# Hybrid attention trunk on one core: where two activation tables come from, when unit 0's heads take ScalarE, and how one matmul triple in a step reads its moving operand

## The chip, the core and the metric

The kernel runs on one core of a Trainium2 chip. The core has TensorE (matmuls), VectorE, ScalarE (activations and copies), GpSimd and SyncE; the last two mostly issue DMAs. In profile rows they are PE (its weight loads PEld), DVE, ACT, POOL and SP. The metric is the time of one execution on the device in microseconds; three executions of the kernel before took 1690.44, 1692.59 and 1696.43 us.

## What is computed

Only layer 0 of the reference exists (DEPTH is 1): an RMSNorm, an attention branch with a residual, and a last RMSNorm. There are 256 rows of 4096 floats, 32 heads of 128.

```python
h = x + attn_branch(rms_norm(x, norm_attn), w_in_attn, w_out_attn)
out = rms_norm(h, final_norm)
# attn_branch: q, k, v, g = split(xn @ w_in, 4)          w_in is 4096 x 16384
z = einsum(q_block, k) * scale                           # one head, strictly causal
log_fail = where(causal, log_sigmoid(-z), 0)
suffix = cumsum(log_fail, axis=3, reverse=True) - log_fail
a = exp(log_sigmoid(z) + suffix)                         # 0 where not causal
o = a @ v
branch = (o * silu(g)) @ w_out                           # w_out is 4096 x 4096
```

All is float32, and the two projections are nearly all of the work.

## The kernel before

**Projections.** Twenty units follow each other on TensorE: units 0 to 15 make columns of q, k, gate and v, two heads each, and units 16 to 19 multiply by w_out. A unit has 16 steps along the contraction. A step works on 2 x 2 blocks; in units 0 and 16 ("plain") it takes 8 products, in the others ("mixed") 7 products in 11 or 9 of the 16 steps, made from sums and differences of blocks (SEVEN_PARTS), and 8 in the rest. One product is a **triple** of matmuls: weights and activations are each split into a rounded high part and a low rest (wh, wl; sh, sl or oh, ol), and the triple is wh with sh, wl with sh, wh with sl, all into one PSUM bank (acc). The weights are the moving operand, 512 columns wide. ScalarE casts the raw weights to wh, VectorE subtracts to get wl and also forms the sums.

**How a triple reads.** mm3 (lines 816 to 822) gives each matmul a read and write order by a letter: with "e" the 512 columns go in groups of eight neighbours, four passes over the row ("128x4x16x8" in the order of instructions), with "c" in groups of four ("128x4x32x4"). product (from line 1245) picks the three letters: the first seven triples behind a heads' group use BEHIND_OTHERS (line 36), else the first triple of a step uses IN_STEP (line 37, by the step's number, even or odd), and all others "eee".

**Heads.** While unit u + 1 runs, the two heads of unit u are worked off between its triples. One head is four groups on TensorE (turn: the transposes; scores; scan: the sums of f, high and low part fh and fl; values) and between them work on ScalarE: a copy, softplus and its scaled copy (f), a cast (fh), Relu and Exp (a), small copies. Each unit also takes one Silu of the gate. Silu, softplus and Exp are in three table sets, so a load of a table (ACT_TABLE_LOAD) stands ahead of Silu, and ahead of softplus and Exp of each head: five a unit, 80 in 16 units. The last heads' group of a unit stands in step 6 of the next one.

**What sets the order.** A planner (class Plan) runs the whole program through costs written in it and emits the instructions in the order that results. Each piece of work for ScalarE or VectorE waits in a heap under a key, a time, and the lowest key goes first. act and dve use soon(), 4 us ahead of TensorE's place, if none is given (lines 327 to 339); casts of weights have the time of their first product, less 2 or 6 us. What the planner emits is fixed: the chip runs each engine's instructions in that order, and each waits for its operands.

**The output part and the end.** plain_h (from line 1075) is unit 16's end: four copies from PSUM to h, one for each bank. The last parts of unit 19 are reordered so that banks 5, 4, 2 and 3 are finished one after the other. With each, block_done adds the bank, ScalarE takes squares with a sum (sq), VectorE joins the sums, and finish (from line 1184) takes r = Exp(-0.5 * Ln(mean)), a Newton step on VectorE, and then the rows of the output are scaled and stored. It does so for rows 128 to 255 first and for rows 0 to 127 after the last bank. Ln and Exp come from different sets there, so each of the two root() calls has a table load ahead of Ln and one ahead of Exp. One load at the program's begin (line 274) asks for a set that has both; the first norm's factor uses it.

All instructions pass through one helper, so the profile gives line 133 for nearly all of them; they are told apart by operation and tile.

Of the kernel before, what the change touches and what calls it, by code (L numbers as in the profile page):

```python
# [13 lines left out]
AF = mybir.ActivationFunctionType  # L14
# [5 lines left out]
P = 128  # L20
S = 256
# [11 lines left out]
EPS = 1e-6  # L33

RUNS = {"e": (4, 8), "c": (4, 4), "g": (2, 8)}
BEHIND_OTHERS = ("ccc", "ecc", "eee", "eee", "eee", "eee", "cce")
IN_STEP = ("cce", "ecc")
BEHIND = {}
WARM, IDLE = 10, 640

# [7 lines left out]
TABLE = 1400  # L48
# [17 lines left out]
H_LATER = 3  # L66
GAIN_LATER = 30.0
ON_SCALAR = ((1, 3, 5), (1, 3))
AHEAD, SUMS_AHEAD = 4.0, 4.0
BLOCKS_LATER = 2  # L70
FORMS_BEHIND = 3
# [34 lines left out]
def scalar_ns(n):  # L106
    return 98 + n / 1.2
# [142 lines left out]
def kernel(  # L250
# [10 lines left out]
    nc = Plan(tc)  # L261
# [14 lines left out]
    def minus(out_, full, part):  # L276
        nc.vector.tensor_tensor(out=out_, in0=full, in1=part.bitcast(F32), op=ALU.subtract)
# [49 lines left out]
    def soon(c=4.0):  # L327
        return nc.here + 1e3 * c


    def dve(emit, n, key=None, more=0, **kw):
        n = n if isinstance(n, tuple) else (n,)
        cost = sum(vector_ns(m) for m in n) + 122 * (len(n) - 1) + more
        return nc.work("vector", cost, emit, soon() if key is None else key, **kw)

    def act(emit, n, key=None, **kw):
        n = n if isinstance(n, tuple) else (n,)
        cost = sum(scalar_ns(m) for m in n) + 100 * (len(n) - 1)
        return nc.work("scalar", cost, emit, soon() if key is None else key, **kw)
# [3 lines left out]

    since_others, words = 0, BEHIND_OTHERS

    def ten(emit, *n, what):
        def others():
            nonlocal since_others, words
            first_ = BEHIND.get(what, ())
            since_others, words = 0, first_ + BEHIND_OTHERS[len(first_) :]  # L350
            emit()

        return nc.work("tensor", 40 + sum(tensor_ns(m) for m in n), others, nc.here - 1e4, wait=400)
# [453 lines left out]
    st, ev = {}, {}  # L807

    def gate(u):
        yield nc.until(("gv", u))  # L810
        g = st["gv", u][:, :, 0:CW]
        n = NT * CW
        yield act(lambda: nc.scalar.activation(g, g, AF.Silu), n + TABLE)
        nc.tell(("gate", u))

    def mm3(out_, a, b, start, stop, orders):
# [8 lines left out]
    BW = 3 * P  # L825
    not_before = off.broadcast_to([P, 2, P])

    def head(u, i):
        yield nc.take("att", "gh", sooner=True)
        tr = att.tile([P, 2, S], F32, tag="att", name=f"tr{u}_{i}")  # L830

        def turn():
            for k in range(2):
                for t in range(NT):
                    c = k * CW + i * P
                    nc.tensor.transpose(tr[:, k, t * P : (t + 1) * P], st["qk", u][:, t, c : c + P], ident)

        yield ten(turn, P, P, P, P, what=("turn", i))
        if i == HG - 1:
            nc.give("one")  # L840
        qk = wp.tile([P, 2, S], F32, tag="gh", name=f"qkT{u}_{i}", bufs=ROWS)
        yield act(lambda: nc.scalar.copy(qk, tr), 2 * S)
        nc.give("att")
        yield nc.take("att", sooner=True)
        bank = att.tile([P, W], F32, tag="att", name=f"z{u}_{i}")
        z, gT = bank[:, 0:BW], bank[:, BW:W]

        def turned(to, t):
            nc.tensor.transpose(to, st["gv", u][:, t, i * P : (i + 1) * P], ident)

        def scores():
            kw = dict(stop=False, skip_group_check=True)
            nc.tensor.matmul(z[:, 0:P], qk[:, 1, P:S], qk[:, 0, P:S], start=True, **kw)
            nc.tensor.matmul(z[:, P:BW], qk[:, 1, 0:P], qk[:, 0, :], start=False, **kw)
            diagonal = z[:, 0 : 2 * P].rearrange("p (a b) -> p a b", a=2)
            nc.tensor.matmul(diagonal, ident_b, not_before, start=False, **kw)

        yield ten(scores, *FULL_P, *FULL_S, 2 * P, what=("scores", i))
        nc.give("gh")
        yield nc.take("gh", sooner=True)  # L860

        f = wp.tile([P, BW], F32, tag="gh", name=f"f{u}_{i}", bufs=ROWS)

        def soft():
            nc.scalar.activation(f, z, AF.Softplus, scale=scale)
            nc.scalar.activation(f, f, AF.Copy, scale=1.0 / scale)

        yield act(soft, (BW + TABLE, BW))
        yield nc.take("gh", "gh", sooner=True)
        fh, fl = (wp.tile([P, BW], F32R, tag="gh", name=f"f{k}{u}_{i}", bufs=ROWS) for k in "hl")  # L870
        yield act(lambda: nc.scalar.copy(fh, f), BW)
        yield dve(lambda: minus(fl, f, fh), BW)
        nc.give("gh")

        if i == 0:
            yield nc.until(("gate", u))

        def scan():
            kw = dict(start=False, skip_group_check=True)
            nc.tensor.matmul(z, neg_tri, fh, stop=False, **kw)  # L880
            nc.tensor.matmul(z, neg_tri, fl, stop=False, **kw)
            nc.tensor.matmul(z[:, 2 * P : BW], neg_one, fh[:, 0:P], stop=False, **kw)
            nc.tensor.matmul(z[:, 2 * P : BW], neg_one, fl[:, 0:P], stop=True, **kw)
            turned(gT, 0)

        yield ten(scan, BW, BW, P, P, P, what=("scan", i))
        nc.give("gh", "gh")
        gated = st["gv", u][:, :, i * P : (i + 1) * P]
        yield nc.take("gh", sooner=True)
        a = wp.tile([P, BW], F32, tag="gh", name=f"a{u}_{i}", bufs=ROWS)  # L890


        def weights_of():
            nc.scalar.activation(a, z, AF.Relu, scale=-scale)
            nc.scalar.activation(a, a, AF.Exp, scale=-1.0)

        yield act(weights_of, (BW, BW + TABLE))
        yield act(lambda: nc.scalar.copy(gated[:, 0, :], gT), P)
        nc.give("att")
        yield nc.take("att", sooner=True)  # L900
        bank2 = att.tile([P, BW], F32, tag="att", name=f"o{u}_{i}")
        o, gT2 = bank2[:, 0:S], bank2[:, S:BW]
        v = lambda t: st["gv", u][:, t, CW + i * P : CW + (i + 1) * P]

        def out_of_head():
            kw = dict(skip_group_check=True)
            nc.tensor.matmul(o, v(0), a[:, P:BW], start=True, stop=False, **kw)
            nc.tensor.matmul(o[:, P:S], v(1), a[:, 0:P], start=False, stop=True, **kw)
            turned(gT2, 1)

        yield ten(out_of_head, *FULL_P, *FULL_S, P, what=("values", i))
        nc.give("gh")
        yield act(lambda: nc.scalar.copy(gated[:, 1, :], gT2), P)
        o2 = o.rearrange("p (t b) -> p t b", t=NT)
        yield dve(lambda: nc.vector.tensor_tensor(out=gated, in0=o2, in1=gated, op=ALU.mult), S)
        nc.give("att")
# [3 lines left out]
    def heads(u):  # L920
        nc.start(gate(u))
        yield nc.until(("qk", u))
        for i in range(HG):
            yield from head(u, i)

        nc.tell(("heads", u))
        spill[u] = dp.tile([P, 4, P], F32, name=f"spill{u}")
        there = spill[u].rearrange("p (i t) b -> p t i b", t=NT)
        here = st["gv", u][:, :, 0:CW].rearrange("p t (i b) -> p t i b", i=HG)

        def out_():
            for t in range(NT):
                nc.gpsimd.dma_start(there[:, t], here[:, t])

        yield moved("gpsimd", out_, [2 * P] * NT, soon(), after=lambda: (nc.give("two"), nc.tell(("spilled", u))))
# [47 lines left out]
    def make_room():  # L983
        nonlocal ep
        rooms.close()
        ep = ctx.enter_context(tc.tile_pool(name="last", bufs=1))
# [87 lines left out]

    def plain_h(u, c):
        yield nc.until(*(("spilled", v) for v in range(NB)), ("full", u, PLAIN["C11"]))
        make_room()
        for k in range(2):
            new_h(c + k)
        for k in range(2):  # L1080
            for t in range(NT):
                b = PLAIN[f"C{t + 1}{k + 1}"]
                yield nc.until(("full", u, b))
                yield act(lambda: nc.scalar.copy(hs[c + k, t], ev[u][b]), W, place_of[u + 1, 0] - 2e3)
                nc.give(f"b{b}")
        nc.tell(("C", u))
# [121 lines left out]
    def rows_out(c, t, f, key):  # L1208
        h = hs[c, t]
        if c >= NJ - 2:  # L1210
# [6 lines left out]
            )  # L1217
        elif c in ON_SCALAR[t]:
            yield act(lambda: nc.scalar.activation(h, h, AF.Copy, scale=f), W, key)
# [25 lines left out]
    def product(n, k):  # L1245
# [7 lines left out]
        elif p["i"] == 0 and k == 0:  # L1253
            orders = IN_STEP[p["s"] % len(IN_STEP)]
        since_others += 1
# [89 lines left out]
```

## Time and profile before

| | |
|---|---|
| median of three executions | 1692.59 us (1690.44 to 1696.43) |
| the profiled execution, its own time | 1690.6 us |
| its span, first to last instruction | 1688.9 us |
| TensorE busy | 1666.1 us, 99% |
| VectorE busy | 1611.2 us, 95% |
| ScalarE busy | 1268.8 us, 75% |
| table loads on ScalarE | 84 and the first one, 1283 ns each |
| DMA | 417 MB, 247 GB/s in the mean |

All durations in the text come from the one profiled execution; between its span and its own time lie 1.7 us, and the median of the three lies 2.0 above its own time. A row such as "L133 ACT CAST wh<-raw 128x1024 x2" is line, engine, operation, what is written from what, shape and count; in timeline rows the start and the duration in us stand ahead, and in brackets the idle time of the engine before it and who ended it. The chain of waits is followed back from the last instruction: each piece is the work or the wait without which the next could not have begun. A matmul's duration in a row overlaps the next one's; its pace is the distance of starts.

### The profile page before, as it was taken

To read this page: it belongs to the slowest core of one execution; us is meant where nothing else is said; L and a number is where in the kernel's file an instruction comes from. 1 tells how busy PE (TensorE), PEld (TensorE's weight loads), DVE (VectorE), ACT (ScalarE), POOL (GpSimd) and SP (SyncE) were. 2 spreads that over 40 slices of the span, in tenths; PEclk is the share of its full clock that TensorE was granted. 3 is DMA by queue.
4 is the path that set the end of the run, shared out by engine and by line. 5 is a ranking of instruction groups with operands and counts; after the bars stand their busy time and mean duration, and the time that the engine had idled before them with its cause. 6 is when DMAs were issued, how large, how long until landed. Compare 5 with 4: busy or idle time off the path is not lost.

```text
span 1688.9 us, 24974 instructions
## 1 busy us (share of the span) xinstructions
PE 1666.1 (99%) x7731; PEld 1409.2 (83%) x7731; DVE 1611.2 (95%) x1851; ACT 1268.8 (75%) x1668; POOL 365.8 (22%) x448
## 2 busy tenths in 40 slices
PE   9999999999999999999999999999999999999995
PEld 7888888888888888888888888888888888888884
DVE  8889999999999999999999999999999978999996
ACT  8886968686868696868686868787878766656665
POOL 0022222222222222222222222222222112212110
PEclk9999999999999999999999999999999999999998
DMA  9968898988897979797979798889888977979894
GB/s 338 349 177 252 230 261 222 259 227 257 228 265 212 274 202 281 199 285 206 272 215 265 215 260 227 247 235 251 231 249 239 291 247 239 274 223 275 249 307 148
DMA packets 253174, 417.22 MB, mean 247 GB/s; under 512 B 28784, under 2 KB 77168, under 8 KB 253040
## 3 DMA queue, kind: packets, MB, share of 16 engines
q1 hardware_dynamic: 194544, 354.24, 62.9%
q0 software_dynamic: 58208, 61.11, 21.9%
q8 instruction: 60, 0.98, 0.2%
q14 instruction: 74, 0.61, 0.1%
q10 hardware_dynamic: 288, 0.28, 0.1%
HBM read 407.13 MB, written 8.39 MB: 246 GB/s over the span
## 4 chain that ended last, share of the span: by engine, by line
PE 93%; DVE 4%; issue 1%; ACT 1%; DMA 1%; SPq 0%; DVEq 0%; ACTq 0%
PE acc L133 88%; PE z L133 3%; DVE wl L133 2%; PE o L133 1%; PE tr L133 1%; DVE h L133 1%; DVE raw L133 1%; DMA raw<-in_w_out_dram 0%; ACT wh L133 0%; DMA xres<-in_x_dram 0%; ACT L133 0%; DMA raw<-in_w_in_dram 0%; DVE wh L133 0%; SPq L133 0%; ACT sq L133 0%
## 5 line engine op out<-in xcount | busy, mean ns | idle before, releaser
L133 ACT CAST wh<-raw 128x1024 fp32r<-128x1024 f32 (+1 forms) x1019 | 936.5, 966 | 326.0 <-PE acc L133 139.3
L133 DVE TENSOR_TENSOR wl<-raw,wh 128x1024 fp32r<-128x1024 f32 (+1 forms) x830 | 989.8, 1219 | 42.8 <-ACT wh L133 19.5
L133 PE MATMUL acc<-wh,sh 128*128 128x512 f32 x2048 | 766.0, 387 | 0.4 <-ACT wh L133 0.4
L133 PE MATMUL acc<-wh,sl 128*128 128x512 f32 x1883 | 721.3, 383 | 0.0
L133 PE MATMUL acc<-wl,sh 128*128 128x512 f32 x1718 | 657.7, 383 | 2.2 <-DVE wl L133 2.2
L133 POOL DMA_DIRECT2D raw<-in_w_in_dram x330 | 284.0, 945 | 1003.5 <-DMA raw<-in_w_in_dram 409.6
L133 PEld LDWEIGHTS acc<-wh,sh 128*128 128x128 f32 x2048 | 384.7, 188 | 70.9 <-ACT wh L133 0.8
L133 PEld LDWEIGHTS acc<-wh,sl 128*128 128x128 f32 x1883 | 352.8, 187 | 63.8 <-DVE sl L133 0.6
L133 PEld LDWEIGHTS acc<-wl,sh 128*128 128x128 f32 x1718 | 322.5, 188 | 58.9 <-DVE wl L133 3.6
L133 DVE TENSOR_TENSOR raw<-raw 128x512 f32<-128x512 f32 x378 | 359.9, 952 | 4.6 <-DMA raw<-in_w_out_dram 1.4
L133 PE MATMUL acc<-wh,oh 128*128 128x512 f32 x512 | 192.1, 383 | 0.0
L133 PE MATMUL acc<-wh,ol 128*128 128x512 f32 x488 | 186.5, 382 | 0.0
L133 PE MATMUL acc<-wl,oh 128*128 128x512 f32 x464 | 177.5, 383 | 1.5 <-DVE wl L133 1.4
L133 DVE TENSOR_TENSOR wh<-raw,wh 128x512 fp32r<-128x512 f32 x189 | 129.3, 684 | 1.4 <-ACT wh L133 1.4
L133 PEld LDWEIGHTS acc<-wh,oh 128*128 128x128 f32 x512 | 96.0, 187 | 17.1
L133 ACT ACT_TABLE_LOAD x84 | 107.8, 1283 | 1.5
L133 PEld LDWEIGHTS acc<-wh,ol 128*128 128x128 f32 x488 | 91.4, 187 | 16.0
L133 PEld LDWEIGHTS acc<-wl,oh 128*128 128x128 f32 x464 | 87.0, 187 | 18.1 <-DVE wl L133 2.8
L133 POOL DMA_DIRECT2D raw<-in_w_out_dram x48 | 41.8, 971 | 161.5 <-DMA raw<-in_w_out_dram 49.9
L133 POOL DMA_DIRECT2D p<-spill x28 | 17.0, 648 | 100.0 <-DVE ol L133 63.8
L133 DVE SCALAR_TENSOR_TENSOR gv_sb<-acc,scalars,gv_sb 128x512 f32<-128x512 f32 x45 | 33.5, 745 | 0.0
L133 ACT CAST oh<-p 128x512 fp32r<-128x512 f32 (+3 forms) x47 | 21.2, 471 | 13.8 <-DVE p L133 13.1
(87 smaller groups left out, 709.5 us busy)
## 6 DMA issues: line engine op xcount, KB each, us to landing
raw<-in_w_in_dram SPq DMA_DIRECT2D x1024, 256.0 KB, 4.5
raw<-in_w_out_dram SPq DMA_DIRECT2D x256, 256.0 KB, 4.4
raw<-in_w_in_dram POOLq DMA_DIRECT2D x330, 128.0 KB, 4.9
p<-spill POOLq DMA_DIRECT2D x28, 256.0 KB, 4.4
raw<-in_w_out_dram POOLq DMA_DIRECT2D x48, 128.0 KB, 5.6
xr<-in_x_dram SPq DMA_DIRECT2D x16, 256.0 KB, 5.1
spill<-gv_sb POOLq DMA_DIRECT2D x32, 128.0 KB, 4.8
xres<-in_x_dram SPq DMA_DIRECT2D x16, 256.0 KB, 5.8
```

The source lines that it names most:

```text
L133: return self.tc.keep_in_program_order(getattr(self.engine, name)(*args, **kw))
```

## The change

Three things. (1) BEHIND_OTHERS's last entry and IN_STEP's first go from "cce" to "ecc": the triple's four-column groups move from the first two matmuls to the last two. In steps with odd numbers IN_STEP was "ecc" already. (2) In unit 0 the ScalarE work of gate and head gets a key 12 us ahead of TensorE's place instead of 4 (HEADS_FIRST); a higher key means later, so casts of weights get in front of it. In the other units it stays at 4. (3) plain_h emits a load of the set that has both Ln and Exp, behind the last heads.

```diff
-BEHIND_OTHERS = ("ccc", "ecc", "eee", "eee", "eee", "eee", "cce")
-IN_STEP = ("cce", "ecc")
+BEHIND_OTHERS = ("ccc", "ecc", "eee", "eee", "eee", "eee", "ecc")
+IN_STEP = ("ecc", "ecc")
...
+HEADS_FIRST = 12.0
...
     def gate(u):
+        act_ = lambda *w: act(*w, soon(4.0 if u else HEADS_FIRST))
...
-        yield act(lambda: nc.scalar.activation(g, g, AF.Silu), n + TABLE)
+        yield act_(lambda: nc.scalar.activation(g, g, AF.Silu), n + TABLE)
...
     def head(u, i):
+        act_ = lambda *w: act(*w, soon(4.0 if u else HEADS_FIRST))
...
-        yield act(soft, (BW + TABLE, BW))
+        yield act_(soft, (BW + TABLE, BW))
...
-        yield act(weights_of, (BW, BW + TABLE))
-        yield act(lambda: nc.scalar.copy(gated[:, 0, :], gT), P)
+        yield act_(weights_of, (BW, BW + TABLE))
+        yield act_(lambda: nc.scalar.copy(gated[:, 0, :], gT), P)
...
     def plain_h(u, c):
         yield nc.until(*(("spilled", v) for v in range(NB)), ("full", u, PLAIN["C11"]))
+        yield act(lambda: nc.scalar.preload_act_table_set("natural_log_exp_and_others"), TABLE)
         make_room()
```

The copies qk, fh and gated[:, 1, :] in head go from act to act_ as well. Three places show what the planner and the placing of loads make of it.

ScalarE at the beginning of unit 1, where unit 0's first head begins; wh36 and wh37 are the casts for the second half of unit 1's step 1, f0_0 is softplus of head 0. Before:

```order
L133 ACT_TABLE_LOAD
L133 ACTIVATE gv_sb0_1045<-gv_sb0_1045 128x2x256
L133 ACT_TABLE_LOAD
L133 ACTIVATE f0_0_1097<-z0_0_1083 128x384
L133 ACTIVATE f0_0_1097<-f0_0_1097 128x384
L133 CAST wh36_1015<-raw_76 128x1024
L133 CAST wh37_1016<-raw_76 128x1024
L133 CAST fh0_0_1118<-f0_0_1097 128x384
L133 CAST wh42_1131<-raw_76 128x1024
```

Now:

```order
L134 ACT_TABLE_LOAD
L134 ACTIVATE gv_sb0_1045<-gv_sb0_1045 128x2x256
L134 CAST wh36_1015<-raw_76 128x1024
L134 CAST wh37_1016<-raw_76 128x1024
L134 ACT_TABLE_LOAD
L134 ACTIVATE f0_0_1097<-z0_0_1083 128x384
L134 ACTIVATE f0_0_1097<-f0_0_1097 128x384
L134 CAST wh42_1135<-raw_76 128x1024
L134 CAST fh0_0_1138<-f0_0_1097 128x384
```

The two casts stand ahead of softplus's load and its two activations; the next cast, wh42, still stands behind them and ahead of fh.

VectorE at the same place; the rows with raw on both sides are sums of weights, and wl36 and wl37 are what TensorE needs first. Before:

```order
L133 TENSOR_TENSOR raw_76<-raw_76 128x2x2x256
L133 TENSOR_TENSOR raw_76<-raw_76 128x2x256
L133 TENSOR_TENSOR wl36_1125<-raw_76,wh36_1015 128x1024
L133 TENSOR_TENSOR raw_76<-raw_76 128x4x256
L133 TENSOR_TENSOR wl37_1133<-raw_76,wh37_1016 128x1024
L133 TENSOR_TENSOR fl0_0_1119<-f0_0_1097,fh0_0_1118 128x384
L133 TENSOR_TENSOR wl42_1145<-raw_76,wh42_1131 128x1024
```

Now:

```order
L134 TENSOR_TENSOR raw_76<-raw_76 128x2x2x256
L134 TENSOR_TENSOR wl36_1110<-raw_76,wh36_1015 128x1024
L134 TENSOR_TENSOR wl37_1117<-raw_76,wh37_1016 128x1024
L134 TENSOR_TENSOR raw_76<-raw_76 128x2x256
L134 TENSOR_TENSOR raw_76<-raw_76 128x4x256
L134 TENSOR_TENSOR wl42_1148<-raw_76,wh42_1135 128x1024
L134 TENSOR_TENSOR fl0_0_1139<-f0_0_1097,fh0_0_1138 128x384
```

One half-size sum moved from ahead of wl36 to behind wl37. On TensorE the scan group of head 0 moved one triple forward in the same step.

ScalarE at the end; sq6_1 and sq7_1 are squares of rows 128 to 255, the two rows with scalars on both sides are Ln and Exp of their root. Before:

```order
L133 ACTIVATE sq7_1_0_15291,squares_of_rows_141<-h7_1_14743 128x512
L133 ACTIVATE sq6_1_0_15297,squares_of_rows_141<-h6_1_14697 128x256
L133 ACTIVATE sq6_1_256_15304,squares_of_rows_141<-h6_1_14697 128x256
L133 ACT_TABLE_LOAD
L133 ACTIVATE scalars_78<-squares_of_rows_141,scalars_78 128x1
L133 ACT_TABLE_LOAD
L133 ACTIVATE scalars_78<-scalars_78 128x1
L133 ACTIVATE sq6_0_0_15322,squares_of_rows_141<-h6_0_14696 128x512
```

Now:

```order
L134 ACTIVATE sq7_1_0_15292,squares_of_rows_141<-h7_1_14744 128x512
L134 ACTIVATE sq6_1_0_15298,squares_of_rows_141<-h6_1_14698 128x256
L134 ACTIVATE sq6_1_256_15305,squares_of_rows_141<-h6_1_14698 128x256
L134 ACTIVATE scalars_78<-squares_of_rows_141,scalars_78 128x1
L134 ACTIVATE scalars_78<-scalars_78 128x1
L134 ACTIVATE sq6_0_0_15323,squares_of_rows_141<-h6_0_14697 128x512
```

The two loads are gone from this root, and from the other one (rows 0 to 127) in the same way. The load that came in stands at unit 16's end, between two casts of oh13 and ahead of the first of the four copies to h; the weight cast wh880, which stood behind the second copy, now stands ahead of it.

More of the change, by code (lines that the diff above doesn't have):

```diff
@@ L841, in head @@
         qk = wp.tile([P, 2, S], F32, tag="gh", name=f"qkT{u}_{i}", bufs=ROWS)
-        yield act(lambda: nc.scalar.copy(qk, tr), 2 * S)
+        yield act_(lambda: nc.scalar.copy(qk, tr), 2 * S)
         nc.give("att")
@@ L866, in soft @@
             nc.scalar.activation(f, f, AF.Copy, scale=1.0 / scale)
-        yield act(soft, (BW + TABLE, BW))
+        yield act_(soft, (BW + TABLE, BW))
         yield nc.take("gh", "gh", sooner=True)
         fh, fl = (wp.tile([P, BW], F32R, tag="gh", name=f"f{k}{u}_{i}", bufs=ROWS) for k in "hl")
-        yield act(lambda: nc.scalar.copy(fh, f), BW)
+        yield act_(lambda: nc.scalar.copy(fh, f), BW)
         yield dve(lambda: minus(fl, f, fh), BW)
@@ L912, in head @@
         nc.give("gh")
-        yield act(lambda: nc.scalar.copy(gated[:, 1, :], gT2), P)
+        yield act_(lambda: nc.scalar.copy(gated[:, 1, :], gT2), P)
         o2 = o.rearrange("p (t b) -> p t b", t=NT)
```

## The prediction

> **What bounds the kernel now.** I read the page first, for shares and for the chain that ended last.
>
> ```profile
> span 1688.9 us, 24974 instructions
> PE 93%; DVE 4%; issue 1%; ACT 1%; DMA 1%; SPq 0%; DVEq 0%; ACTq 0%
> L133 ACT ACT_TABLE_LOAD x84 | 107.8, 1283 | 1.5
> ```
>
> TensorE carries 93% of the chain; what is left is 7%, and the change can win only there. The 84 table loads on ScalarE take 107.8 us, so what counts is which of them stand on the chain. The second view is therefore the chain in order of time: a mixed unit in the middle, and then the end.
>
> ```profile
> 878.03 47.60 PE acc L133 x216
> ```
>
> This is the long stretch behind the last heads' group of a mixed unit: TensorE alone is on the chain, at 47.60 / 216 = 0.2204 us a matmul. No wait can be taken away there, only pace.
>
> ```profile
> 1667.19 0.45 ACT sq L133 x2
> ...
> 1667.72 1.28 ACT L133
> 1669.01 0.29 ACT scalars L133
> 1669.33 1.28 ACT L133
> 1670.62 0.21 ACT scalars L133
> 1670.86 0.23 DVE scalars L133
> ...
> 1675.92 1.28 ACT L133
> ...
> 1677.53 1.28 ACT L133
> ```
>
> At the end four table loads are links of the chain: one ahead of Ln and one ahead of Exp, for each half of the rows. The second pair begins after TensorE's last matmul (below), and nothing hides it.
>
> The third view is the timeline of unit 1's beginning, on VectorE, ScalarE and TensorE in turn; it is the one place outside the end where the change moves instructions and TensorE waits.
>
> ```profile
> 93.80 2.55 DVE L133 TENSOR_TENSOR raw<-raw 128x512 f32<-128x512 f32 x3
> 99.62 1.23 DVE L133 TENSOR_TENSOR wl<-raw,wh 128x1024 fp32r<-128x1024 f32 x1 [3.28 <-ACT wh L133]
> ```
>
> ```profile
> 95.67 0.63 ACT L133 ACTIVATE gv_sb<-gv_sb 128x512 f32<-128x512 f32 x1
> ```
>
> ```profile
> 123.44 0.43 PE L133 MATMUL acc<-wh,sh 128*128 128x512 f32 x1
> 125.22 0.51 PE L133 MATMUL acc<-wl,sh 128*128 128x512 f32 x1 [1.35 <-DVE wl L133]
> ```
>
> VectorE stands 3.28 us for a cast that ScalarE has put behind the heads' activations, and TensorE pays 24 us later: from 123.44 to 125.22 is 1.78, less one matmul of 0.22, so 1.56 lost.
>
> **The change part by part.** *Table loads at the end, first pair (rows 128 to 255).*
>
> ```profile
> 1668.26 0.15 DVE L133 SCALAR_TENSOR_TENSOR scalars<-squares_of_rows,scalars 128x1 f32<-128x1 f32 x1
> ...
> 1674.06 0.75 DVE L133 TENSOR_TENSOR h<-acc,h 128x256 f32<-128x256 f32 x2
> ```
>
> ```profile
> 1671.19 0.40 PE L133 MATMUL acc<-wh,ol 128*128 128x512 f32 x1
> ```
>
> With the set that holds Ln and Exp already loaded, two steps of 1.29 (1669.01 - 1667.72, 1670.62 - 1669.33) go: Exp ends at 1670.83 - 2.58 = 1668.25. Then another operand is late: VectorE's sum ends at 1668.41, so Newton's step starts at 1668.45 instead of 1670.86, 2.41 earlier. VectorE works without a break from there to the additions of the last bank at 1674.06, 3.20 later, so these could start at 1671.65. TensorE's last matmul ends at 1671.19 + 0.40 = 1671.59: the gain of 2.41 has 0.06 us to spare, and TensorE is what is late next.
>
> *Second pair (rows 0 to 127).* Nothing else is on ScalarE there, and the sum that Newton's step also needs is done while the loads run. Both steps go whole, 2 x 1.29 = 2.58. Together 4.99 us.
>
> The output transfers could take some of that back, so I looked at the windows of the last microseconds (busy us of TensorE, its weight loads, VectorE, ScalarE, GpSimd; then clock, DMA share, GB/s).
>
> ```profile
> 1676.00:1678.00 2.00, 0.00 (x0) 0.00 (x0) 0.09 (x1) 1.97 (x3) 0.00 (x0) 0.67 0.80 297
> ...
> 1680.00:1682.00 2.00, 0.00 (x0) 0.00 (x0) 1.96 (x6) 1.85 (x3) 0.00 (x0) 0.50 0.56 206
> ```
>
> The first half's stores are through by about 1677.6 (1676 + 0.80 x 2); the second half's begin to move data near 1680.9 (1682 - 0.56 x 2). The first wave moves up by 2.41, to an end at 1675.2, the second by 4.99, to a beginning at 1675.9. They stay apart by 0.7 us. If that cover were gone, the loss is what overlaps, some tenths. So 4.99, with 2.6 as the low end if the first pair were lost, and nothing above 5.2 (4 x 1.29).
>
> The row gives a load 1.28 us, and Ln follows it at 1.29; ahead of it, from 1667.64 to 1667.72, next to nothing is lost. The Trainium skill, "ScalarE: Activation LUTs", section "What ACT_TABLE_LOAD costs", adds a drain of about 1380 ns to the 1283 ns, 2.66 us for every switch; by it the four would be worth an estimated 10.6 us in place of 4.99. The trace disagrees: no such drain stands between these rows.
>
> *Later heads in unit 0.* The order of ScalarE shows both casts of the second half of step 1 ahead of the softplus pair. They can start when Silu ends, 95.67 + 0.63 = 96.30.
>
> ```profile
> 96.32 1.28 ACT L133 ACT_TABLE_LOAD   x1
> ...
> 98.56 1.98 ACT L133 CAST wh<-raw 128x1024 fp32r<-128x1024 f32 x2
> ```
>
> That is 98.56 - 96.30 = 2.26 earlier, and VectorE's idle 3.28 shrinks by as much. Not all of it arrives at 125 us. One half-size sum, the last third of the x3 row at 93.80 (2.55 less 0.69 and 1.22, some 0.6), ran in that idle time and now stands behind the two subtractions. And the next cast, which now follows the load, softplus and its copy, ends near 96.30 + 1.98 + 2.24 + 1.0 = 101.5 (2.24 from the load's start to the casts' in the rows above), while VectorE, begun at 99.62 - 2.26 = 97.36 with three steps of some 1.15 and the sum of 0.6 to do, is free for it at 101.4: up to 0.2 of waiting. That leaves 2.26 - 0.6 - 0.2 = 1.45.
>
> ```profile
> 99.00:123.00 24.00, 24.00 (x115) 19.91 (x114) 23.38 (x26) 20.80 (x28) 3.42 (x4) 1.00 0.68 192
> ```
>
> VectorE is busy 23.38 of the 24 us in between, with the same work in nearly the same order before and after, so the 1.45 reaches the subtraction that ends TensorE's wait. TensorE itself arrives a little sooner and waits a tenth or some more; it goes on 1.45 earlier. Bounds: -2.3 if the whole head start counts; +0.5 if TensorE's groups of unit 0's heads, now behind casts of 0.99 each, keep TensorE waiting. The nearest to that is scan, which needs fl:
>
> ```profile
> 103.04 0.55 DVE L133 TENSOR_TENSOR fl<-f,fh 128x384 fp32r<-128x384 f32 x1
> ```
>
> ```profile
> 104.43 0.34 PE L133 MATMUL z<-fh,neg_tri 128*128 128x384 f32 x1
> ```
>
> With an end at 103.59 there is 104.43 - 103.59 = 0.84 us to spare; the new order puts it one triple (0.66) sooner, and fl comes near 101.5 + 1.15 + 0.55 = 103.2, 0.4 sooner: some 0.4 stays after TensorE's own small gain. I take -1.45, the end that the VectorE rows lead to.
>
> *The added load in the output part.* It runs behind the cast at 1426.31, and ScalarE then idles anyway.
>
> ```profile
> 1426.31 0.51 ACT L133 CAST oh<-p 128x384 fp32r<-128x384 f32 x1 [0.78 <-DVE p L133]
> 1427.70 0.59 ACT L133 COPY h<-acc 128x512 f32<-128x512 f32 x1 [0.88 <-PE acc L133]
> ```
>
> 0.88 of its 1.28 lies in that wait; the copies that free the banks come some 0.4 to 0.7 late, and in the new order the next weight cast stands ahead of the second copy, so VectorE gets it on time. Cost 0; 1.28 if the cover is gone. Small swaps on VectorE and SyncE follow it. They could touch the place where TensorE waits later:
>
> ```profile
> 1545.00:1572.00 27.00, 25.78 (x115) 21.17 (x114) 27.00 (x30) 18.17 (x23) 6.29 (x8) 1.00 0.82 223
> ```
>
> That is 27.00 - 25.78 = 1.22 us of TensorE idle beside a VectorE that never rests. I leave it as it is: 0, between -1.2 and the +1.28 of an uncovered load.
>
> *The read orders.* The same three matmuls, two of them in groups of four before and after; only which two moves, in about half of the steps and behind each heads' group. The long stretch has 9 such triples and loses against an even 0.22 a matmul 47.60 - 47.52 = 0.08 us. If all of it went, or doubled, in 16 units, that is -1.3 or +1.3; the before has both forms in turn in that stretch, so I take 0.
>
> Sum: 2.41 + 2.58 + 1.45 = 6.44. The profiled execution took 1690.6, so 1684.2 of its kind; the median of the three runs shown is 1692.59, 2.0 above it, and gives 1686.2. About 0.3%, 5.1 us, is what a measurement of this kernel can tell from no change.
>
> **The rivals.** *A, unit 1 gives nothing:* the wait at 125 us goes but comes back at a group of unit 0's heads. For it speaks the thin cover ahead of scan; against it that VectorE is the late one in all of that stretch. 1692.6 - 5.0 = 1687.6.
>
> *B, the first pair is lost* to the last bank or to the stores, which have 0.06 and 0.7 us to spare: 1692.6 - 2.58 - 1.45 = 1688.6.
>
> *C, slower: TensorE's pace.* Behind a stall in unit 0 the trace shows another pace than 0.2204:
>
> ```profile
> 36.08 0.39 PE L133 MATMUL acc<-wl,sh 128*128 128x512 f32 x1
> ...
> 38.38 0.39 PE L133 MATMUL acc<-wh,sl 128*128 128x512 f32 x1
> ```
>
> Ten matmuls in 2.30 us, 0.230 each. If the read in four, four, eight is what ends that pace and eight, four, four doesn't, each long stretch behind the heads costs 216 x 0.0096 = 2.1 us. Three stretches eat the gain, from the sixth on the kernel is slower by over 5.1; all 15 give 1692.6 - 6.4 + 31 = 1717. Against it: odd steps have eight, four, four already, and the long stretch holds 0.2204.
>
> *D, the loads come back:* the tool that builds the program may place its own loads whatever is asked for. Then 1692.6 - 1.45 = 1691.1. In the order they are gone, and the 84 + 1 loads of before stood in its order just as in the trace. The Trainium skill, "ScalarE activation tables: per-element evaluation and per-set limits", section "Table sets in the compiler and the runtime", says the back end places the loads, by the longest run; no run here shows it yet for this set.
>
> *E, a drain goes with each load.* Ahead of the first one the chain has room for 0.08 us at most (1667.64, where the accumulators end, to 1667.72); four of them give 1686.2 - 0.3 = 1685.9. The skill's section on the load's cost would make it an estimated 1680.5; the 0.08 speaks against that.
>
> **How the numbers follow.** Forecast 0.68, A 0.13, B 0.07, C 0.06, D 0.04, E 0.02. Of the forecast's 0.68 some 0.04 may end under 5.1 us of gain, since it clears that by only 1.3. Faster: 0.64 + E = 0.66. Same: 0.04 + A + B + D = 0.28. Slower: C, 0.06. The time is the forecast's, 1686.2. The range goes down to 1682.0 (unit 1 at -2.3, a part of the open 1.2 and 1.3, and runs that lie as low against the median as the profiled one) and up to 1690.5 (A and B with the added load uncovered); C and D lie outside.
>
> **What would show it.** On the chain at the end: no ScalarE step of 1.28; additions of the last bank within 0.1 of TensorE's end; about 12.3 us from there to the end of the span, where it is 14.8 now from 1674.06. 82 loads in place of 85 on ScalarE. In unit 1: VectorE's wait near 96 us at about 1.0, TensorE's near 123 under 0.6. In the mixed units 0.2204 a matmul as before. The prediction is wrong if a group of unit 0's heads is on the chain with a ScalarE wait ahead of it, if a load still stands ahead of Ln or Exp, or if the long stretches change by more than 0.1 us each.

## The result, and the profile after

| | before | after |
|---|---|---|
| median of six executions | 1693.51 us (1690.44 to 1696.66) | 1684.1 us (1683.72 to 1685.36) |
| the profiled execution, its own time | 1690.6 us | 1685.3 us |
| its span | 1688.9 us | 1683.6 us |

The ratio is 0.9942, with a 95% interval of 0.9927 to 0.9958: 9.4 us less by the medians, where 6.4 was forecast. The two profiled executions differ by 5.3 us only. So the first question is what these two pairs of numbers don't share. One thing shows already: the six times of before are spread over 6.2 us, those of after over 1.6.

The page of after, its span, the shares of its chain and the table loads:

```profile
span 1683.6 us, 24973 instructions
PE 95%; DVE 2%; DMA 1%; issue 1%; ACT 0%; DVEq 0%; POOL 0%; SPq 0%; ACTq 0%; POOLq 0%
L134 ACT ACT_TABLE_LOAD x81 | 103.9, 1283 | 1.5
```

Three loads fewer (four gone, one added), and ScalarE's share of the chain reads 0% in place of 1%. The end of the chain:

```profile
1668.08 0.16 DVE scalars L134
...
1668.35 0.23 DVE scalars L134
...
1672.06 0.53 ACT sq L134 x2
...
1673.16 0.30 ACT scalars L134
1673.46 0.02 issue
1673.48 0.21 ACT scalars L134
1673.70 0.02 issue
1673.72 0.23 DVE scalars L134
```

Ln and Exp follow each other with 0.02 us between them; no step of 1.28 is left. The row at 1668.35 is Newton's first step of rows 128 to 255, and the chain comes to it from VectorE's sum at 1668.08, not from Exp. The timeline of the same microseconds, VectorE's work ahead of the last bank, its additions, and TensorE's last matmul:

```profile
1670.89 0.75 DVE L134 SCALAR_TENSOR_TENSOR h<-h,scalars,grow 128x512 f32<-128x512 f32 x1
1671.55 0.74 DVE L134 TENSOR_TENSOR h<-acc,h 128x256 f32<-128x256 f32 x2
```

```profile
1671.02 0.40 PE L134 MATMUL acc<-wh,ol 128*128 128x512 f32 x1
```

From the last matmul's start to the end of the span it was 1688.89 - 1671.19 = 17.70 us and is 1683.57 - 1671.02 = 12.55: 5.15 less. The additions begin 0.13 us after TensorE's end (1671.42), but it isn't TensorE that they wait for: no idle time of VectorE stands ahead of them, and 3.20 us lie from Newton's step to them (1671.55 - 1668.35), as many as before (1674.06 - 1670.86). VectorE is late here, and TensorE has 0.13 us to spare.

The beginning of unit 1, ScalarE, VectorE and TensorE:

```profile
96.71 1.98 ACT L134 CAST wh<-raw 128x1024 fp32r<-128x1024 f32 x2
98.70 1.28 ACT L134 ACT_TABLE_LOAD   x1
```

```profile
97.77 2.36 DVE L134 TENSOR_TENSOR wl<-raw,wh 128x1024 fp32r<-128x1024 f32 x2 [1.52 <-ACT wh L134]
```

```profile
123.38 0.39 PE L134 MATMUL acc<-wh,sh 128*128 128x512 f32 x1
124.21 0.50 PE L134 MATMUL acc<-wl,sh 128*128 128x512 f32 x1 [0.44 <-DVE wl L134]
```

The casts are ahead of the load, VectorE stands 1.52 us where it stood 3.28, and TensorE loses 124.21 - 123.38 - 0.22 = 0.61 us where it lost 1.56. Last, the long stretch of a mixed unit with what stands ahead of it, before and after, as pieces of the chain:

```profile
456.74 5.36 PE acc L133 x24
462.10 0.76 PE o L133 x5
462.86 47.60 PE acc L133 x216
```

```profile
455.65 5.33 PE acc L134 x24
460.99 0.76 PE o L134 x5
461.75 47.67 PE acc L134 x216
```

47.67 / 216 = 0.2207 us a matmul, 0.07 us a unit more than before. By these two executions the read orders are worth nothing.

Where the 5.3 us between the two profiled executions lie, by the starts of the first matmul of each unit in the two traces: the end 5.15, unit 1 1.49 (85.14 to 83.65), units 2 to 15 together 0.15, unit 0 0.52, unit 19 0.08; against that the first matmul starts 1.03 later, and units 17 and 18 take 1.03 more, in waits for weights and the pace behind them. That the change causes these last two isn't shown: a second profile of the unchanged kernel before (below) has units 17 and 18 1.4 us shorter than the first, so they vary by as much without it.

### The profile page after: what moved, and what is told of

The parts are those of the page before. It is cut to its first block, busy times and chain, and to the rows that moved or that the text cites. A ratio compares the mean times of both kernels' runs of the same rounds, so it can differ in the third digit from the quotient of the medians.

```text
span 1683.6 us, 24973 instructions
## 1 busy us (share of the span) xinstructions
PE 1666.7 (99%) x7731; PEld 1410.6 (84%) x7731; DVE 1611.0 (96%) x1851; ACT 1265.0 (75%) x1665; POOL 365.9 (22%) x448
## 4 chain that ended last, share of the span: by engine, by line
PE 95%; DVE 2%; DMA 1%; issue 1%; ACT 0%; DVEq 0%; POOL 0%; SPq 0%; ACTq 0%; POOLq 0%
PE acc L134 90%; PE z L134 3%; PE o L134 1%; DVE wl L134 1%; PE tr L134 1%; DMA raw<-in_w_out_dram 1%; DVE raw L134 0%; DVE h L134 0%; ACT wh L134 0%; DMA raw<-in_w_in_dram 0%; DVE scalars L134 0%; DVE wh L134 0%; ACT sq L134 0%; ACT scalars L134 0%; POOL raw L134 0%
```

## The experiments

The theory after the result: the end and unit 1 went as forecast, and the 3 us beyond it come from the read orders. The rival: they come from the other two parts or from the sample of before. Each kernel was compared with the kernel before on the same chip.

| kernel | median, us | lowest to highest | ratio and interval |
|---|---|---|---|
| orders_only | 1691.39 | 1690.33 to 1692.46 | 0.9976 [0.9966, 0.9985] |
| load_only | 1691.89 | 1686.40 to 1693.32 | 0.9972 [0.9961, 0.9983] |
| heads_only | 1694.93 | 1694.12 to 1696.43 | 0.9997 [0.9988, 1.0006] |
| without_orders | 1690.91 | 1689.93 to 1692.63 | 0.9973 [0.9964, 0.9982] |
| after | 1684.1 | 1683.72 to 1685.36 | 0.9942 [0.9927, 0.9958] |
| seventh_only | 1684.09 | 1682.76 to 1684.35 | 0.9929 [0.9912, 0.9946] |
| steps_only | 1690.37 | 1686.57 to 1691.94 | 0.9974 [0.9960, 0.9987] |
| no_fours | 1691.68 | 1688.83 to 1693.64 | 0.9980 [0.9968, 0.9992] |
| parity | 1682.82 | 1681.62 to 1683.38 | 0.9923 [0.9906, 0.9940] |
| even_all | 1684.51 | 1683.43 to 1685.24 | 0.9940 [0.9921, 0.9959] |

**orders_only.** The kernel before with the two tables of the read order from after:

```diff
-BEHIND_OTHERS = ("ccc", "ecc", "eee", "eee", "eee", "eee", "cce")
-IN_STEP = ("cce", "ecc")
+BEHIND_OTHERS = ("ccc", "ecc", "eee", "eee", "eee", "eee", "ecc")
+IN_STEP = ("ecc", "ecc")
```

> Only the read orders change: eight, four, four at each step's begin and as the seventh triple behind a heads' group. Theory (each part adds what its rows show): the matmul rows of the two traces differ by 0.2 us in unit 0 and 0.03 us in each mixed unit, so 0.6 us faster in all, and the times keep the spread of the kernel before (6 us). Rival (the 3 us by which the medians differ beyond the profiled executions come from the read orders): 3 to 4 us faster in the median, spread under 2 us.

4.7 us less by the medians (1696.11 to 1691.39). But its fastest execution, 1690.33, is no faster than the fastest of before, 1690.16 of all; only the spread went, from 6.4 us (1691.70 to 1698.07) to 2.1. The traces agree: units 2 to 15 together take 1161.6 us here and 1161.9 in the first profile of before. The orders don't make a good execution faster; they remove the bad ones.

**load_only.** The kernel before with the added load alone:

```diff
     def plain_h(u, c):
         yield nc.until(...)
+        yield act(lambda: nc.scalar.preload_act_table_set("natural_log_exp_and_others"), TABLE)
```

> Only the added table load at unit 16's end. Theory: 5.0 us faster, all of it behind TensorE's last matmul, where 17.7 us of the span become 12.6; the spread of the times stays that of the kernel before. Rival (the unexplained 3 us hang on the load): 8 us faster with a spread under 2 us.

4.2 us less, and the spread stays, 6.9 us. From the last matmul to the end its trace has 12.56 us: all of the end's gain belongs to the load. Yet its profiled execution took 1690.34, only 0.3 less than the profiled one of before. The chain shows where the gain went:

```profile
707.33 0.66 PE z L133 x5
707.99 5.52 PE acc L133 x24
713.51 0.76 PE o L133 x5
714.28 47.85 PE acc L133 x216
```

Against before's 5.36 and 47.60 that is 0.41 us a unit. The 24 matmuls between scan and values of the second head go at 5.52 / 24 = 0.230 us, the pace that rival C had found in unit 0, and the 0.25 more in the long stretch is some 25 matmuls at that pace, by the trace its first ones. Units 2 to 14 of this execution take 83.40 or 83.41 us each, where before has 83.01 (83.12 in unit 8); unit 15 takes 83.03 for 82.65.

**heads_only.** The kernel before with HEADS_FIRST and act_ alone:

```diff
+HEADS_FIRST = 12.0
...
+        act_ = lambda *w: act(*w, soon(4.0 if u else HEADS_FIRST))
```

> Only unit 0's heads later on ScalarE. Theory: 1.5 us faster, TensorE's wait near 123 us falls from 1.56 to 0.6 and the small losses of steps 1 to 3 in unit 1 go. Rival (the unexplained 3 us come from unit 1, where the kernel before runs with a tenth of a us to spare): 4 to 5 us faster with a spread under 2 us.

0.5 us less by ratio, within the interval of nothing. In the trace unit 1 does take 83.54 us in place of 85.14, 1.6 less, and TensorE waits as in after:

```profile
123.78 0.50 PE L134 MATMUL acc<-wl,sh 128*128 128x512 f32 x1 [0.41 <-DVE wl L134]
```

But units 2 to 14 take 83.40 us each here as well, and units 2 to 15 together 5.3 us more than in the first profile of before; all eleven executions lie over 1694. A gain of 1.5 us can't be seen beside that.

**without_orders.** The kernel after with the two tables of before (the first diff, the other way round).

> The whole change but for the read orders, which stay four, four, eight in even steps. Theory: 6.5 us faster. If the unexplained 3 us belong to the read orders, 6 us faster with a spread of 6 us; if they belong to the heads or to the load, 9 us faster with a spread under 2 us, as the whole change.

5.2 us less than before, 0.31% short of what after gained. Its trace has both other gains (12.55 us at the end, 83.53 in unit 1) and 83.40 us in the mixed units. So the orders are worth some 5 us of the whole, in executions that would else have units of 83.40.

With that a sharper theory: with the old orders TensorE has two ways through a mixed unit, 83.01 or 83.40 us; an execution is on one or the other from unit 2 or 3 to unit 15, and under the new orders none stays on the long one. (In the profiled execution of after, unit 10 alone took 83.25 us, and unit 11 83.01 again.) At the entry to the lost stretch, in step 5, only the seventh triple differs between the old order and the new. So it should be the seventh; the rival is the step's begin.

**seventh_only.** After, with IN_STEP as before:

```diff
-IN_STEP = ("ecc", "ecc")
+IN_STEP = ("cce", "ecc")
```

> The kernel after, but the first triple of an even step reads four, four, eight again (IN_STEP as before); only the seventh triple behind a heads' group keeps the new order. In the profiles with the old orders two kinds of mixed units were seen: units of 83.01 us (the kernel before as profiled) and units of 83.40 us (three of the experiments), with the 0.39 us lost in steps 5 and 6, between the last two heads' groups, at 0.230 us a matmul. Theory: the seventh triple decides, since at the entry to that stretch it is the only one that the edit changes. Then this kernel's units stay at 83.0 us and it takes 1684.1, within 1 us of the kernel after. Rival: the triple at the begin of even steps decides; then its units come to 83.4 us and it takes 1687 to 1690. Second rival: either alone does; then this one is like the kernel after too, and so is the next.

1684.09 with a spread of 1.6 us, as after. The transposes of the two heads of a unit show its period on the chain (the first and the third row are one unit apart):

```profile
426.59 0.44 PE tr L134 x4
445.90 0.44 PE tr L134 x4
509.53 0.44 PE tr L134 x4
```

509.53 - 426.59 = 82.94 us. The edit of IN_STEP does nothing that the times can tell. In the traces these units are 0.05 us shorter than those of after (82.93 to 82.99 in most), which the run parity explains.

**steps_only.** After, with the seventh triple of before:

```diff
-BEHIND_OTHERS = ("ccc", "ecc", "eee", "eee", "eee", "eee", "ecc")
+BEHIND_OTHERS = ("ccc", "ecc", "eee", "eee", "eee", "eee", "cce")
```

> The kernel after, but the seventh triple behind a heads' group reads four, four, eight again; the step's first triple keeps the new order in all steps. Theory (the seventh decides): its units can fall to 83.4 us, and it takes up to 1689.5 (14 units by 0.39 us more than 1684.1), in any case over 1686. Rival (the step's begin decides): units of 83.0 us and 1684.1, within 1 us.

1690.37, 0.9 over the most that was expected, and the spread is back: 1686.57 (the profiled one, units of 83.04 us), then nine from 1689.08 to 1691.94. So between seventh_only and this kernel the seventh decides. That the slow nine had long units was an inference still, as their traces weren't taken; the next two runs looked.

**before_again** and **steps_again.** The kernel before and steps_only, unchanged, each for a second profile.

> The kernel before once more, unchanged, for a second profile. Its times so far lie in two groups, 1690.2 to 1692.6 and 1694.4 to 1699.8 us, and its one profile (1690.6) has mixed units of 83.01 us. Theory: the two groups are the two ways in which TensorE goes through steps 5 and 6; an execution of over 1694 has units of 83.40 us from early on (14 by 0.39 is 5.5 us), one under 1693 has units of 83.01. Rival: the groups come from something else (transfers at the begin, the waits in the output part), and the units are 83.0 in an execution of over 1694 as well.

> The kernel with the step's begin as after and the seventh triple as before, once more, for a second profile. Its ten times were 1686.6 for the profiled execution, with units of 83.04 us, and 1689.1 to 1691.9 for the others. Theory: an execution of over 1689 has units of 83.4 us in steps 5 and 6 in most units; one under 1687.5 has 83.0. Rival: units of 83.0 in either, and the 4 us lie in waits of the output part or at the begin.

This execution of before took 1694.65 us, and its chain reads

```profile
428.67 0.44 PE tr L133 x4
...
457.93 5.53 PE acc L133 x24
463.45 0.76 PE o L133 x5
464.21 47.85 PE acc L133 x216
512.07 0.44 PE tr L133 x4
```

512.07 - 428.67 = 83.40 us; the first profile of the same program had 510.46 - 427.45 = 83.01 by these rows:

```profile
427.45 0.44 PE tr L133 x4
...
510.46 0.44 PE tr L133 x4
```

steps_again took 1691.19, 4.6 us more than its twin's 1686.57:

```profile
707.26 5.53 PE acc L134 x24
712.78 0.76 PE o L134 x5
713.55 47.88 PE acc L134 x216
```

The theory's numbers were met to 0.03 us (83.43 in steps_again). One program, one order of instructions, two periods. Over the 69 executions of before that these comparisons hold, 21 lie at 1690.2 to 1692.8 (median 1691.7), one at 1693.4 and 47 at 1694.3 to 1699.8 (median 1696.6): by these times, and with one trace from each group, two in three took the long way. The medians are 4.9 apart, where 14 units at 0.39 make 5.5. Within a group the parts show what their rows say: orders_only, with short units in its trace, has its median (1691.39) at that of the lower group, and heads_only, with long ones, is 1.7 us under that of the upper.

How busy the transfers are doesn't tell the two ways apart. In the lost stretch of the second profile (464.2 to 470.0 us) the DMA engines are busy 79% of the time, in the same stretch of the first (462.9 to 470.0) 83%, and the granted clock is 1.00 in both.

**no_fours.** After, with groups of eight in all triples but the first two behind a heads' group:

```diff
-BEHIND_OTHERS = ("ccc", "ecc", "eee", "eee", "eee", "eee", "ecc")
-IN_STEP = ("ecc", "ecc")
+BEHIND_OTHERS = ("ccc", "ecc", "eee", "eee", "eee", "eee", "eee")
+IN_STEP = ("eee", "eee")
```

> The kernel after, but the seventh triple and the step's first triple read in groups of eight only (eee); groups of four are left in the first two triples behind a heads' group. Theory: groups of four are what ends TensorE's 0.230 us pace, and without them a unit that comes out of its heads at 0.230 stays there to the end of the unit: 216 matmuls by 0.0096 us, 2.1 us in each unit that is caught, up to 15 units, so up to 1715; with none caught, 1682 to 1684, since a triple with groups of four costs 0 or 0.013 us itself. Rival: the pace ends by itself, and the fours do nothing but cost 0.013 us here and there: 1682 to 1684.5 with no stretch at 0.230.

7.6 us over seventh_only on the same chip, which took what after takes. The chain of unit 0, and that of the last units, first here and then after:

```profile
19.89 76.11 PE acc L134 x330
...
1579.81 91.35 PE acc L134 x396
```

```profile
19.79 73.23 PE acc L134 x331
...
1579.99 87.46 PE acc L134 x397
```

76.11 / 330 = 0.2306 and 91.35 / 396 = 0.2307 us a matmul, against 0.2212 and 0.2203: behind the waits at the begin and in unit 18 TensorE stays at the slower pace for 330 matmuls on end, where no group of four stands. For as many matmuls after needs 3.1 us less in unit 0 and 4.1 less at the end. In after the pace starts at a wait in unit 0 too, but by the starts of the matmuls it is over within seven matmuls behind the next pair in groups of four, some 30 in all; in before, where that pair has the other order, it ends in the same way. The transfers aren't the reason: over these stretches of unit 0 the DMA engines are busy 95% of the time here and 98% in after, with a granted clock of 1.00 in both.

The theory held for these units alone. The mixed units of this profile took 82.85 to 82.95 us from unit 2 to 14, and no stretch at 0.230 shows in them: they never fell into the pace, so whether it ends by itself there isn't shown. The profiled execution took 1689.06 and others up to 1693.64; where those lost more wasn't seen.

With this the lost stretch of before_again can be read again. Behind scan, the seventh triple's pair of fours comes as the 19th and 20th of 24 matmuls, and four matmuls later the values group cuts in. Behind it the pace is there again, and ends seven matmuls behind the next seventh triple's pair: some 49 matmuls in each of the units 2 to 15, and none there in the first profile of before.

**parity.** The intervals between matmul starts in the traces show what one pair of matmuls in fours costs inside a long stretch: nothing when the number of matmuls from the last such pair is even (24, a step of eight products; 67 of the 70 such places in after), 0.013 to 0.015 us when it is odd (21, a step of seven; 108 of 114). This kernel is after with the form chosen so that the distance is even:

```diff
-IN_STEP = ("ecc", "ecc")
+IN_STEP = ("ecc", "cce")
...
-            orders = IN_STEP[p["s"] % len(IN_STEP)]
+            orders = IN_STEP[since_others % len(IN_STEP)]
```

> The kernel after, but the first triple of a step reads four, four, eight when its number behind the last heads' group is odd, eight, four, four when it is even, so that the number of matmuls from one pair of fours to the next is always even. Theory: by the intervals of the profiles such a pair costs nothing where that distance is even (24, a step of eight products) and 0.013 us where it is odd (21, a step of seven); some 6 pairs in each of 16 units lose it in the kernel after, 0.08 us a unit, and this kernel takes 1.2 us less, 1682.9, with units of 82.91 us. Rival: the 0.013 us belongs to the order (eight, four, four), not to the distance: then about half of it stays and the time is 1683.5. Second rival: with four, four, eight at some steps the units can fall to 83.4 us: 1689.

1682.82 us, 1.3 less than seventh_only on the same chip, where 1.2 was expected against after. The two intervals overlap nearly whole (0.9923 [0.9906, 0.9940] and 0.9929 [0.9912, 0.9946]), and of the 1.3 us the two traces have only 0.4 in units 2 to 15, so the times don't show it and the trace has to:

```profile
709.62 47.58 PE acc L134 x216
```

47.58 against 47.67 in after: 0.09 us a unit, where six pairs at 0.013 make 0.08. Both forms cost nothing here, and in before both cost 0.014 at odd distances, so in the long stretch it is the distance and not the form. Of all kernels this one has the lowest median.

**even_all.** parity with the seventh triple in four, four, eight again, and even distances from the second triple behind the heads on:

```diff
-BEHIND_OTHERS = ("ccc", "ecc", "eee", "eee", "eee", "eee", "ecc")
-IN_STEP = ("ecc", "cce")
+BEHIND_OTHERS = ("ccc", "ecc", "eee", "eee", "eee", "eee", "cce")
+IN_STEP = ("cce", "ecc")
```

> As the kernel with even distances, but with the seventh triple in four, four, eight, and the step's first triple so chosen that every distance between pairs of fours is even from the second triple behind the heads on (14 matmuls to the seventh, where eight, four, four makes 15). Theory: the seventh's own form decides whether steps 5 and 6 can fall into the 0.230 us pace; then this kernel is spread over 4 us or more and its median lies over 1685, like the other kernels with that form. Rival: what decides is the distances; then it is at 1682.5, with a spread of under 2 us, and units of 82.9 us.

Here the theory of the seventh's own form fell. The kernel differs from without_orders, all of whose eleven executions lay at 1689.9 or more, in one line only, the one that picks the form of a step's first triple. It has the seventh triple of before, and lies at 1684.51 with a spread of 1.8 us and units of 82.95 and 82.97 in turn; the row of its transposes over three units:

```profile
L134 PE MATMUL tr<-ident,qk_sb x28: 269/271/273, 343.2 to 592.4; 128*128 128x128 f32 x28
```

592.4 - 343.2 is 249.2, less 0.3 for the place in the group, by three: 82.96. If it took the long way as often as before does, six executions in a row without it would come up about once in 400 to 700 times (4 in 11 on this chip, or a third, to the sixth power). So what keeps TensorE out of the long way is the sequence of forms and distances around the heads, not the seventh triple by itself. The rival's number, 1682.5, wasn't met either: its units 2 to 15 lose 0.4 us in all against those of parity. The starts of the matmuls name a place for it, and a limit of the rule of distances. The seventh triple's pair, 14 matmuls behind the second triple's, costs 0.014 us in 61 of 81 places here, though 14 is even; in parity, at 15, it costs nothing in 63 of 67. So close behind the heads the rule doesn't hold.

## Why the prediction was right, and where it was not

**Loads at the end, 2.41 + 2.58.** Measured 5.15 for 4.99. From the last matmul's start to Newton's first step of rows 128 to 255 it was -0.33 us and is -2.67: 2.34 (the row at 1668.35 above). VectorE's sum is the operand that is late, as forecast. The forecast had the additions wait for VectorE and TensorE next in line; so it is, with 0.13 us to spare where 0.06 was worked out. The second pair brought 2.81. ScalarE's timeline there, before and after:

```profile
1674.85 0.39 ACT L133 ACTIVATE sq<-h 128x256 f32<-128x256 f32 x1 [1.57 <-DVE h L133]
...
1675.71 0.19 ACT L133 ACTIVATION_READ_ACCUMULATOR sq<-h 128x1 f32 x1
1675.92 1.28 ACT L133 ACT_TABLE_LOAD   x1
...
1678.82 0.20 ACT L133 ACTIVATE scalars<-scalars 128x1 f32<-128x1 f32 x1
```

```profile
1672.06 0.39 ACT L134 ACTIVATE sq<-h 128x256 f32<-128x256 f32 x1 [1.29 <-DVE h L134]
...
1672.94 0.19 ACT L134 ACTIVATION_READ_ACCUMULATOR sq<-h 128x1 f32 x1
1673.16 0.29 ACT L134 ACTIVATE scalars<-squares_of_rows,scalars 128x1 f32<-128x1 f32 x1
1673.48 0.20 ACT L134 ACTIVATE scalars<-scalars 128x1 f32<-128x1 f32 x1
```

From the squares to Exp it was 3.97 us and is 1.42: 2.55 for the two loads. Another 0.28, which the sum didn't have, lies between the first addition of the last bank and its squares (0.79, now 0.51). The chain up to the squares names the place:

```profile
1673.09 1.73 DVE h L133 x4
```

```profile
1670.58 1.40 DVE h L134 x3
```

Before, the squares begin behind both additions (1674.82), now behind the first of them (1671.98). The traces without the added load have 0.78 or 0.79 and those with it 0.51 or 0.52; why the wait moved isn't shown. Ahead of the load 0.02 us pass behind the accumulator's end (1675.90), ahead of Ln without a load 0.03 (1673.13). So nothing of a drain goes with the load. The Trainium skill, "ScalarE: Activation LUTs", section "What ACT_TABLE_LOAD costs", has one of about 1380 ns; these rows don't show it, and rival E is out. Rivals B and D are out by the same rows.

**Later heads, 1.45.** Measured 1.49 in unit 1, and 1.6 with that part alone. TensorE's wait shrinks by 0.95 of it; for the rest TensorE comes there some 0.55 us sooner, mainly because some 40 matmuls that ran at 0.230 us behind an earlier, small wait no longer do. VectorE waits 1.52 near 96 us, not the 1.0 that the text listed: that figure left out the half-size sum of 0.6, which the term itself had taken off. Rival A is out.

**The added load, and TensorE's waits in the output part, 0 each.** Unit 16, at whose end the load stands, takes 90.23 us in both traces. In units 17 and 18 the waits vary by 1.4 us between two executions of the same kernel before, and by as much among kernels with and without the load. Nothing can be put down to it; 0 isn't contradicted, but what the load might cost behind unit 16 could not have been seen.

**The read orders, 0.** This is the term that was mis-sized. The step that failed is "the before has both forms in turn in that stretch, so I take 0", and with it the bounds of 1.3. In an execution on the long way it is worth 5.5 us (units 2 to 15 take 1167.2 us in before_again and 1161.8 in after), on the short way 0.15. The working looked at the long stretch of one execution, which happened to be on the short way, and took its 0.2204 us for the kernel's pace; the loss lies in steps 5 and 6, and in two executions of three. By the sign that the prediction gave itself, a long stretch that changes by more than 0.1 us, it holds for one way only: 47.60 to 47.67, but 47.85 to 47.67 on the other. Rival C had the pace of 0.230 us that hangs on the order of reads, and the wrong sign: under the old orders executions stay in it. Its reason, that one form ends the pace and the other doesn't, fell with even_all and with unit 0, where either form ends it. What could have told before the result was the spread of the three times, 6 us; the text set it aside as 2.0 us between profile and median.

So the sum reads: 6.6 us (5.15 and 1.49) from what the terms named, and from units 2 to 15 0.15 on the short way and 5.5 on the long. From the lower group of before, 1691.7, that gives 1684.9; from the upper, 1696.6, it gives 1684.5. Measured were 1684.1 for after. How far the forecast of 6.4 lay from the measured 9.4 is in part luck: three of the six executions of before fell into each group, so their median lies between the groups. Six from the lower one would have shown some 7.6 us, six from the upper 12.5.

What stays open: why TensorE holds one of two paces through some fifty matmuls with all operands there, and what sends an execution on the one or the other way in unit 2. The runs show which sequences of reads allow the long way, not what in the chip does it.

## What to carry to other kernels

If the times of a kernel fall into two groups, take a second profile before pricing anything: a term worked out from one execution holds for its group only. When ScalarE ends the program with functions of different table sets, a load of the one set that has them all, placed where ScalarE idles, takes every switch off the end, here at no price that could be measured. A change of a read pattern isn't free merely because both patterns are in use already: what follows what, and at which distance, can set the pace.

## What the runs showed of the hardware

TensorE runs these 512-column matmuls at 0.2203 to 0.2207 us or at 0.2306, with all operands ready and a granted clock of 1.00 in either case. Behind a wait it can fall into the slower pace and stay there: for 330 matmuls in unit 0 of no_fours, where all later ones read in groups of eight (76.11 us), for some 30 in after, where pairs in groups of four are strewn in (73.23 for 331).

In the long stretches a pair of matmuls in groups of four between others in groups of eight costs 0.013 to 0.015 us when the number of matmuls from the last pair to it is odd, and nothing when it is even; with even distances a stretch of 47.67 us got 0.09 shorter. For the first pair behind the heads this doesn't hold: it cost 0.014 at a distance of 14 and mostly nothing at 15.

Such a path outlives the work around it: from unit 3 to unit 14, some 1000 us, one execution of before keeps to a period of 83.40 us and another to 83.01, to 0.01 us but for one unit of 83.12, though the program is the same.
